# Earlier and later loads at three places of a decoder layer on one core

## The chip, the cores and the metric

The kernel runs on one core of one Trainium2 chip. The time is device microseconds of one execution; the median of three runs stands for a kernel. The engines are TensorE (PE, with its weight loads PEld), VectorE (DVE), ScalarE (ACT), GpSimd (POOL) and SyncE (SP). Each of them takes its instructions in a fixed order. SP does no arithmetic here: it issues most of the transfers (queue q1 of the profile). POOL issues the rest (queue q0).

## The reference

One decoder layer over 256 tokens of 2048 channels, in float32:

```
h = layer_norm(ALPHA * x + 0.5 * swiglu(x, w_gate1, w_up1, w_down1))       # norm 1
c_q, c_kv, k_r, dq, dk, dv, gate_mla, gate_diff = split(h @ w_in)
o_mla  = mla_attention(rms_norm(c_q) @ w_uq, rms_norm(c_kv) @ w_uk, ... @ w_uv)
o_diff = diff_attention(dq, dk, dv)
y      = sigmoid(gate_mla) * (o_mla @ w_br_mla) + sigmoid(gate_diff) * (o_diff @ w_br_diff)
h = layer_norm(ALPHA * h + y @ w_out)                                       # norm 2
h = layer_norm(ALPHA * h + 0.5 * swiglu(h, w_gate2, w_up2, w_down2))       # norm 3
```

The compressed rows are c_q and c_kv, 512 columns each, which go through an RMS norm and then into `w_uq`, `w_uk` and `w_uv`.

## The kernel before, in words

**Units.** All weights pass through the chip once, in units of two 128-row slices of 512 columns: 512 KB (`project`, L216). For each unit the kernel loads 128x1024 floats into a `raw` buffer (4 of them, SP issues, L235), splits them into a high and a low half (`split`, L153: ACT casts to the high half on L154, DVE subtracts it from the source on L155) into a pair of the ring (`wring`), and multiplies: each product of a 128x128 activation tile with 512 columns is three matmuls, high by high, high by low and low by high (`triple`, L207 to L210). A unit serves 256 tokens as two halves of 128, so `project` has 12 matmuls for each unit, 6 for a half. Where the products go through seven combined forms (`Hybrid`, L351), a unit of a form has 6.

**Order.** The order of work is set in three ways. First, the code is traced unit by unit: `unit` (L194) loads, and `advance` then prepares (casts) and multiplies units that are `look`ed ahead by a given number. Each unit multiplied is one tick; `later(n, fn)` (L103) puts a step n ticks on. Second, the framework plans a static order for each engine and queue from these instructions: one that is ready, and for which a buffer is free, may be placed ahead of others. Third, `tc.issue_after(ins)` puts an instruction behind `ins` on the same engine, in order only. `fetched[0]` is the last weight transfer traced.

**Buffers.** The `tmp` tag has 6 buffers of 128x512 floats, shared by everything that is short-lived: a row block on its way out (`blocks`), one on its way back (`turned`), rows of a product (`dkTr`), gain and shift rows (`gp`). A turn of a 128x512 block goes through DRAM: DVE transposes 32x32 blocks (L715), POOL stores them in four transfers (L717), and POOL reads them back in one (`turned`, L729 or L1227).

**The start.** `xT`, the transposed input, comes in four quads of 512 channels, for two token halves each (`load_x`, L1399; tile `xraw`, then split into `x`). `first_tokens` and `second_tokens` call it within the first projection of feed-forward 1. In that projection unit 0 is loaded and split in two halves (`parts`, L230), every other unit whole. Quad 0 serves units 0 and 1, quad 1 serves units 2 and 3.

**The compressed rows.** After their RMS norm, c_q and c_kv are stored turned. `c_back` (L1224), in the mixer, reads the four blocks back, 6 ticks after the `dk` projection has been traced; `cn.put` (L1231) splits them 12, 14, 16 and 18 ticks after. At that point seven units are loaded or cast and not yet multiplied. The `dv` projection, 22 units, lies between this and the first product with `cn` (`w_uq`).

**Norm 2.** While `w_out` is multiplied (4 column blocks of 512, 8 units each), the object `LayerNorm` (L739) prepares the residual. `rows` (L756, transfer on L764) loads rows of h, four blocks of 128x1024 (tile `z`), and `gained` (L766) loads the gain and shift rows of norm 1 for 512 columns (tile `gp`, the same 2 KB for all 128 partitions, transfer on L770), and multiplies, adds and scales (`use`, L772 to L777). The calls take their ticks from the constructor on L1425: rows at 1, 3, 11, 13; `gained` at 2, 7, 14, 21; `use` 4 and 6 ticks after `gained`. The transfers are put behind the last weight transfer traced. For the first columns `use` also waits until the last quad of y has been split (`past`). Just before, in the last branch projection (`om`), the merged rows `diff` are made by DVE (L1374 to L1376) and turned: two quads through DRAM (`turned`, split into `y`), the last two by PE with an identity matrix (L671).

Of the kernel before, what the change touches and what calls it, by code (L numbers as in the profile page):

```python
# [30 lines left out]
G = 2  # L31
# [28 lines left out]
def layer_kernel(ctx: ExitStack, tc: tile.TileContext, a: dict, out: bass.AP):  # L60
    nc = tc.nc
# [10 lines left out]
    def nm(s):  # L72
        uid[0] += 1
        return f"{s}_{uid[0]}"
# [10 lines left out]
    def mm_bank(name="mm"):  # L85
        return psum.tile([P, 512], F32, tag="mm", name=nm(name), bufs=5)
# [16 lines left out]
    def later(n, fn):  # L103
        uid[0] += 1
        heapq.heappush(todo, (step[0] + n, uid[0], fn))
# [42 lines left out]
            assert (k, b) in self.ready, (self.name, k, b)  # L148
            return self.tiles[k // 8, b][which][:, k % 8, :]

    cast, lows, fetched = [None], [None], [None]

    def split(hi, lo, src):  # L153
        cast[0] = S.copy(hi, src)  # L154
        lows[0] = V.tensor_tensor(out=lo, in0=src, in1=hi.bitcast(F32), op=ALU.subtract)  # L155
        return lows[0]
# [37 lines left out]
    def unit(load, prep, now, later_on=None):  # L194
        if load is not None:
            load()
        loaded.append((prep, now, later_on))
        advance(*ahead)

    def next_pair():  # L200
        assert len(ring) > len(prepared) + lag[0], (len(ring), len(prepared), lag[0])
        catch_up(len(ring) - 1)
        pair = ring.pop(0)
        ring.append(pair)
        return pair

    def triple(o, xh, xl, wh, wl, first, last, again=False):  # L207
        PE.matmul(o, xh, wh, start=first, stop=False, skip_group_check=again)  # L208
        PE.matmul(o, xh, wl, start=False, stop=False, skip_group_check=again)  # L209
        PE.matmul(o, xl, wh, start=False, stop=last, skip_group_check=again)  # L210

    def project(w, x, k_tiles, width, done, k0=0, hook=None, between=None, norm=None, free=(3, 7)):
        banks = [None, None]
        units = k_tiles // G

        def products(b, j, pair):  # L216
            if j == 0:
                banks[b] = mm_bank()
            o = banks[b][:, :width]
            wh, wl = pair  # L220
            for g in range(G):
                k = j * G + g
                xk = k0 + k
                triple(o, x.at(0, xk, b), x.at(1, xk, b), wh[:, g, :], wl[:, g, :], k == 0, k == k_tiles - 1)
            if j == units - 1:
                done(b, banks[b])

        def one(j):
            st = {}
            parts = [slice(i * width, (i + 1) * width) for i in range(G)] if between is not None and j == 0 else [slice(0, G * width)]  # L230

            def load():
                st["raw"] = wpool.tile([P, G * width], F32, tag="raw", name=nm("raw"), bufs=4)
                for c in parts:
                    fetched[0] = nc.sync.dma_start(st["raw"][:, c], w[j][:, c])  # L235

            def prep():
                pair = [t[:, :G * width] for t in next_pair()]
                waits = ()
                if norm is not None and j >= free[0]:  # L240
                    if j >= free[1]:
                        waits = norm.applied[1], norm.root[1]
                    else:
                        waits = norm.x.made[0, 0], norm.root[0] if j == free[0] else norm.x.cast[0, 0]
                with ExitStack() as stack:
                    for i in waits:
                        stack.enter_context(tc.issue_after(i.ins))
                    for c in parts:
                        split(*(t[:, c] for t in pair), st["raw"][:, c])
                st["pair"] = [t.rearrange("p (g n) -> p g n", g=G) for t in pair]  # L250
            def second():
                if between is not None:
                    between(j)
                products(1, j, st["pair"])
            return load, prep, lambda: products(0, j, st["pair"]), second

        for j in range(units):
            if hook is not None:
                hook(j)
            unit(*one(j))  # L260
# [459 lines left out]
    def turned(v):  # L720
        return v.rearrange("p (i k c) -> p k i c", i=4, k=4)
# [17 lines left out]
    class LayerNorm:  # L739
        def __init__(self, scale, residual, g, bt, each, x=None, cols=None, at=((0, 2, 4, 6), (8, 11, 14, 17)), ahead=None, pending=None, due=(), past=None):  # L740
            self.scale = scale
            self.ahead = ahead
            self.x = x
            self.cols = None
            if cols is not None:
                t = tmp_tile([P, 2, KD], "cols")
                nc.gpsimd.dma_start(t.rearrange("p a k -> p (a k)"), cols)
                self.cols = [t[:, i, :] for i in range(2)]
            self.each = each
            self.z = [[None, None] for _ in range(2)]  # L750
            self.counted = [0, 0]
            self.gb = [[None, None] for _ in range(2)]
            self.applied = {}
            self.root = []

            def rows(h, b):  # L756
                t = self.z[b][h] = act_tile([P, 1024], F32, "z")
                src = residual[b, :, h * 1024:(h + 1) * 1024]
                if pending is None:
                    nc.gpsimd.dma_start(t, src)  # L760
                    later(4, lambda: S.mul(t, t, ALPHA))
                else:
                    with tc.issue_after(fetched[0].ins):
                        nc.sync.dma_start(t, src)  # L764

            def gained(c):  # L766
                v = [tmp_tile([P, 512], "gp") for _ in range(2)]
                for t, src in zip(v, pending):
                    with tc.issue_after(fetched[0].ins):
                        nc.sync.dma_start(t, src[0:1, c * 512:(c + 1) * 512].partition_broadcast(P))  # L770

                def use(b):  # L772
                    z = self.z[b][c // 2][:, (c % 2) * 512:(c % 2) * 512 + 512]
                    with tc.issue_after((past() if past is not None and c == 0 else lows[0]).ins):
                        V.tensor_tensor(out=z, in0=z, in1=v[0], op=ALU.mult)
                    V.tensor_tensor(out=z, in0=z, in1=v[1], op=ALU.add)
                    S.mul(z, z, ALPHA)  # L777
                later(4, lambda: use(0))
                later(6, lambda: use(1))
            for c, n in enumerate(due):  # L780
                later(n, lambda c=c: gained(c))

            def vector(i, h):
                t = self.gb[i][h] = act_tile([P, 1024], F32, "gb")
                nc.gpsimd.dma_start(t, (g, bt)[i][0:1, h * 1024:(h + 1) * 1024].partition_broadcast(P))
            for n in range(4):
                later(at[0][n], lambda n=n: rows(n // 2, n % 2))
                if cols is None:
                    later(at[1][n], lambda n=n: vector(n // 2, n % 2))
            self.stats = [small.tile([P, 4, 6], F32, tag="bn", name=nm("bn"), bufs=4) for _ in range(2)]  # L790
# [340 lines left out]
    def mixer(x):  # L1131
# [4 lines left out]
        cn = Acts(8, "cn")  # L1136
# [66 lines left out]
        for i, f in ((0, 0), (1, 0), (0, 2)):  # L1203
            w = (a["wgm"], a["wgd"])[i]
# [17 lines left out]
        back = {}  # L1222

        def c_back():  # L1224
            for key, src in turns.items():
                back[key] = tmp_tile([P, 512], "turned")
                nc.gpsimd.dma_start(back[key], src)  # L1227
        later(6, c_back)
        for i in range(2):
            for b in range(2):  # L1230
                later(12 + 4 * i + 2 * b, lambda i=i, b=b: cn.put(i, b, turned(back[i, b])))  # L1231
        hy.group(a["wdv"][0], a["wdv"][1], lambda n, b, bank, snap, op: whole(
            dv[b][:, n * 512:(n + 1) * 512], bank, snap, op), False, True)
        look(0, 0)
# [125 lines left out]
        yq = Acts(KD, "y")  # L1360
# [34 lines left out]
    res = [dram.tile([2, P, D], F32, name=f"res{i}") for i in range(2)]  # L1395
# [2 lines left out]

    def load_x(q, b):  # L1399
        raw = xq.raw(q, b) if q in xq.kept else tmp_tile([P, 512], "xraw")  # L1400
        nc.sync.dma_start(raw, a["xT"][q, b])
        xq.put(q, b, raw.rearrange("p (k t) -> p k t", k=4))

    def first_tokens(j):
# [9 lines left out]
    def keep(i):  # L1414
        def each(b, c, z):
            nc.gpsimd.dma_start(res[i][b, :, c * 512:(c + 1) * 512], z)
        return each
# [4 lines left out]
    yq = mixer(h1)  # L1422
    narrow_to(6)
    h2 = Acts(KD, "h2", (0, 1, 2))
    ln = LayerNorm(1.0, res[0], a["ln2_g"], a["ln2_b"], keep(1), h2, a["ln2_cols"], ((1, 3, 11, 13), ()), 1,  # L1425
                   (a["ln1_g"], a["ln1_b"]), (2, 7, 14, 21), lambda: yq.made[3, 1])
    for c in range(4):
        project(a["w_out"][c], yq, KD, 512, lambda b, bank, c=c: ln.evac(c, b, bank),
                hook=at_unit(0, widen) if c == 3 else None)
# [90 lines left out]
```

## Time and profile before

| what | us |
|---|---|
| median of 3 runs | 1966.95 (1966.76 to 1967.8) |
| the profiled execution | 1969.03 |
| its span, first to last instruction | 1967.3 |

A row of the timeline gives the start, the duration, the engine, the line, the operation with its tiles (out<-in) and shapes, and a count; in square brackets stands how long the engine was idle before it, and on what. A matmul row can last longer than the distance to the next one, as matmuls are pipelined: the distance of the starts is what one costs. A row of the waits names the engine and the operation that waited, what it waited for, the sum in us, the number of times and the longest. A row of the windows gives, for a stretch, its length, the busy time of PE, PEld, DVE, ACT and POOL with the instructions of each, the granted clock of PE, the share of the transfer engines and GB/s. SPq and POOLq are the queues on which SP and POOL issue transfers.

### The profile page before, as it was taken

What the parts mean: (1) busy time and instruction counts of PE and PEld (TensorE: products, weight loads), DVE (VectorE), ACT (ScalarE), POOL (GpSimd) and SP (SyncE); (2) the same over time, 40 slices, a digit from 0 to 9 for tenths busy, and PEclk for the clock granted to TensorE, in tenths of its full rate; (3) what the DMA queues carried; (4) which work ended last, traced back from release to release, by engine and by line L of the source; (5) the groups of instructions that cost most, each with busy time, mean ns of one, the idle gap of its engine ahead of it and who ended that gap; (6) DMA issues with size and microseconds to landing.
All of it is one profiled execution on the core that took longest, in us unless ns stands there. A gap on an engine that the chain in (4) does not pass through costs nothing.

```text
span 1967.3 us, 25772 instructions
## 1 busy us (share of the span) xinstructions
PE 1951.7 (99%) x8760; PEld 1618.2 (82%) x8760; DVE 1777.8 (90%) x2183; ACT 1249.7 (64%) x1634; POOL 309.3 (16%) x531
## 2 busy tenths in 40 slices
PE   9999999999999999999999999999999999999997
PEld 8888888888888898888888887888888888888886
DVE  7999999998998879988987676789999999999986
ACT  6666766676655666666667654556676666765661
POOL 0112111122100010102241530001211112210000
PEclk9999999999999999999999999999999999999999
DMA  8978888878776666767685788678888878787773
GB/s 315 285 227 262 268 261 247 259 234 306 271 238 214 208 223 248 246 223 262 203 248 196 236 295 274 198 261 255 255 267 264 250 238 271 251 314 236 277 233 121
DMA packets 149779, 488.83 MB, mean 248 GB/s; under 512 B 21600, under 2 KB 21648, under 8 KB 149648
## 3 DMA queue, kind: packets, MB, share of 16 engines
q1 hardware_dynamic: 119088, 401.13, 59.5%
q0 software_dynamic: 30560, 86.07, 16.8%
q8 instruction: 68, 1.11, 0.2%
q14 instruction: 63, 0.52, 0.1%
HBM read 456.71 MB, written 30.41 MB: 248 GB/s over the span
## 4 chain that ended last, share of the span: by engine, by line
PE 92%; DMA 3%; DVE 1%; issue 1%; ACT 1%; POOL 1%; SPq 0%; DVEq 0%; POOLq 0%; ACTq 0%
PE mm L209 29%; PE mm L208 29%; PE mm L210 29%; DMA turned<-turn 1%; DMA gate<-gates 1%; PE tr L210 1%; PE tr L209 1%; PE tr L208 1%; DMA turn<-blocks 0%; POOL turn L717 0%; PE tr L671 0%; ACT wring L154 0%; DMA raw<-in_wgd_dram 0%; DMA raw<-in_gu_dram 0%; PE tr L1322 0%
## 5 line engine op out<-in xcount | busy, mean ns | idle before, releaser
L154 ACT CAST wring<-raw 128x1024 fp32r<-128x1024 f32 (+2 forms) x467 | 481.9, 1037 | 322.3 <-PE mm L210 236.7
L155 DVE TENSOR_TENSOR wring<-raw,wring 128x1024 fp32r<-128x1024 f32 (+2 forms) x467 | 557.4, 1201 | 91.7 <-ACT wring L154 89.4
L154 ACT CAST wring<-sraw 128x1024 fp32r<-128x1024 f32 x436 | 453.0, 1052 | 201.9 <-DVE sraw L428 85.7
L155 DVE TENSOR_TENSOR wring<-sraw,wring 128x1024 fp32r<-128x1024 f32 x436 | 520.7, 1219 | 23.6 <-ACT wring L154 20.7
L208 PE MATMUL mm<-wring,h 128*128 128x512 f32 (+2 forms) x1248 | 480.9, 385 | 0.0
L210 PE MATMUL mm<-wring,h 128*128 128x512 f32 (+2 forms) x1248 | 480.3, 385 | 0.0
L209 PE MATMUL mm<-wring,h 128*128 128x512 f32 (+2 forms) x1248 | 480.0, 385 | 0.0
L208 PE MATMUL mm<-wring,xs 128*128 128x512 f32 x776 | 302.2, 389 | 0.6 <-ACT snap L385 0.6
L209 PE MATMUL mm<-wring,xs 128*128 128x512 f32 x776 | 301.9, 389 | 0.0
L210 PE MATMUL mm<-wring,xs 128*128 128x512 f32 x776 | 301.9, 389 | 0.0
L208 PEld LDWEIGHTS mm<-wring,h 128*128 128x128 f32 x1248 | 234.5, 188 | 46.9 <-ACT h L154 0.6
L209 PEld LDWEIGHTS mm<-wring,h 128*128 128x128 f32 x1248 | 234.5, 188 | 46.5 <-DVE wring L155 0.4
L210 PEld LDWEIGHTS mm<-wring,h 128*128 128x128 f32 x1248 | 234.4, 188 | 46.5 <-DVE h L155 0.7
L428 DVE TENSOR_TENSOR sraw<-sraw,sraw 128x1024 f32<-128x1024 f32 x168 | 199.2, 1219 | 2.0 <-DMA sraw<-in_wgm_dram 1.2
L208 PEld LDWEIGHTS mm<-wring,xs 128*128 128x128 f32 x776 | 145.7, 188 | 31.2 <-ACT snap L385 1.0
L210 PEld LDWEIGHTS mm<-wring,xs 128*128 128x128 f32 x776 | 145.7, 188 | 30.2
L209 PEld LDWEIGHTS mm<-wring,xs 128*128 128x128 f32 x776 | 145.7, 188 | 30.1
L717 POOL DMA_DIRECT2D hT<-blocks x176 | 96.8, 562 | 367.0 <-DVE blocks L715 366.0
L209 PE MATMUL mm<-wring,x 128*128 128x512 f32 x336 | 130.8, 389 | 0.5 <-DVE wring L155 0.5
L208 PE MATMUL mm<-wring,x 128*128 128x512 f32 x336 | 130.8, 390 | 0.0
L210 PE MATMUL mm<-wring,x 128*128 128x512 f32 x336 | 130.6, 389 | 0.0
L430 POOL DMA_DIRECT2D sraw<-in_gu_dram x40 | 35.5, 889 | 371.3 <-DVE sraw L428 288.3
(310 smaller groups left out, 2286.7 us busy)
## 6 DMA issues: line engine op xcount, KB each, us to landing
sraw<-in_gu_dram SPq DMA_DIRECT2D x160, 512.0 KB, 5.2
raw<-in_gu_dram SPq DMA_DIRECT2D x159, 512.0 KB, 4.9
raw<-in_dn_dram SPq DMA_DIRECT2D x140, 512.0 KB, 4.7
sraw<-in_gu_dram POOLq DMA_DIRECT2D x40, 512.0 KB, 7.1
sraw<-in_dn_dram SPq DMA_DIRECT2D x36, 512.0 KB, 5.2
eraw<-in_gu_dram SPq DMA_DIRECT2D x64, 256.0 KB, 5.8
raw<-in_w_out_dram SPq DMA_DIRECT2D x32, 512.0 KB, 4.3
hraw<-hT POOLq DMA_DIRECT2D x56, 256.0 KB, 5.8
```

What stands on the lines that cost most here:

```text
L154: cast[0] = S.copy(hi, src)
L155: lows[0] = V.tensor_tensor(out=lo, in0=src, in1=hi.bitcast(F32), op=ALU.subtract)
L208: PE.matmul(o, xh, wh, start=first, stop=False, skip_group_check=again)
L209: PE.matmul(o, xh, wl, start=False, stop=False, skip_group_check=again)
L210: PE.matmul(o, xl, wh, start=False, stop=last, skip_group_check=again)
L428: last = V.tensor_tensor(out=R[src][i], in0=R[src][i], in1=R[add[1]][i], op=ALU.add)
L430: nc.gpsimd.dma_start(R["12"][s], source("22", s), accum_op=ALU.add)
L717: nc.gpsimd.dma_start(to.rearrange("(g r) (i f) -> i r g f", g=4, i=4)[i], t[32 * i:32 * (i + 1), :].rearrange("r (g f) -> r g f", g=4))
```

## The change

At the start, unit 1 too is loaded and split in halves, and unit 3's transfer is put behind the last transfer of x that has been traced (x's second quad). In the mixer, the reads of the compressed rows move from 6 to 12 ticks, and their splits from 12 to 18. In norm 2, the first two row loads move from ticks 1 and 3 to 2 and 4, the first two `gained` from 2 and 7 to 3 and 8; `use` of the first columns follows 3 and 5 ticks after instead of 4 and 6, so that it keeps its place.

```diff
-            parts = [slice(i * width, (i + 1) * width) for i in range(G)] if between is not None and j == 0 else [slice(0, G * width)]
+            parts = [slice(i * width, (i + 1) * width) for i in range(G)] if between is not None and j < 2 else [slice(0, G * width)]
...
-                for c in parts:
-                    fetched[0] = nc.sync.dma_start(st["raw"][:, c], w[j][:, c])
+                with tc.issue_after(placed[0].ins) if between is not None and j == 3 else nullcontext():
+                    for c in parts:
+                        fetched[0] = nc.sync.dma_start(st["raw"][:, c], w[j][:, c])
...
-                later(4, lambda: use(0))
-                later(6, lambda: use(1))
+                wait = 3 if past is not None and c == 0 else 4
+                later(wait, lambda: use(0))
+                later(wait + 2, lambda: use(1))
...
-        later(6, c_back)
+        later(12, c_back)
...
-                later(12 + 4 * i + 2 * b, lambda i=i, b=b: cn.put(i, b, turned(back[i, b])))
+                later(18 + 4 * i + 2 * b, lambda i=i, b=b: cn.put(i, b, turned(back[i, b])))
...
-        nc.sync.dma_start(raw, a["xT"][q, b])
+        placed[0] = nc.sync.dma_start(raw, a["xT"][q, b])
...
-    ln = LayerNorm(1.0, res[0], a["ln2_g"], a["ln2_b"], keep(1), h2, a["ln2_cols"], ((1, 3, 11, 13), ()), 1,
-                   (a["ln1_g"], a["ln1_b"]), (2, 7, 14, 21), lambda: yq.made[3, 1])
+    ln = LayerNorm(1.0, res[0], a["ln2_g"], a["ln2_b"], keep(1), h2, a["ln2_cols"], ((2, 4, 11, 13), ()), 1,
+                   (a["ln1_g"], a["ln1_b"]), (3, 8, 14, 21), lambda: yq.made[3, 1])
```

More of the change, by code (lines that the diff above doesn't have):

```diff
@@ L149, in at @@
             return self.tiles[k // 8, b][which][:, k % 8, :]
-    cast, lows, fetched = [None], [None], [None]
+    cast, lows, fetched, placed = [None], [None], [None], [None]
     def split(hi, lo, src):
```

## The prediction

> **What bounds the kernel now.** I read the page first, then the waits of TensorE, then the timeline around each of them.
>
> ```profile
> span 1967.3 us, 25772 instructions
> PE 1951.7 (99%) x8760; PEld 1618.2 (82%) x8760; DVE 1777.8 (90%) x2183; ACT 1249.7 (64%) x1634; POOL 309.3 (16%) x531
> ...
> PE tr L671 <- DVE diff L1376: 1.8, 1, 1.8
> ...
> PE mm L208 <- ACT snap L385: 0.6, 1, 0.6
> PE mm L209 <- DVE wring L155: 0.5, 1, 0.5
> ```
>
> TensorE (PE) is busy for 99% of the span, and everything else is cover for it. No row of PE work is added or removed by the change, so it can only win where PE waits, and that list is short. Beside two small ones that the diff does not touch it holds these three, and each lies beside one part of the change. Their real size is read from the starts of neighbouring matmuls:
>
> ```profile
> 9.20 0.63 PE L208 MATMUL mm<-wring,x 128*128 128x512 f32 x2
> 10.36 0.50 PE L209 MATMUL mm<-wring,x 128*128 128x512 f32 x1 [0.53 <-DVE wring L155]
> ...
> 957.67 0.39 PE L210 MATMUL mm<-wring,h 128*128 128x512 f32 x1
> 958.66 0.50 PE L208 MATMUL mm<-wring,xs 128*128 128x512 f32 x1 [0.61 <-ACT snap L385]
> ...
> 1185.03 0.39 PE L209 MATMUL mm<-wring,om 128*128 128x512 f32 x1
> 1185.25 0.39 PE L210 MATMUL mm<-wring,om 128*128 128x512 f32 x1
> 1187.49 0.63 PE L671 MATMUL tr<-ident,diff 128*128 128x128 f32 x4 [1.84 <-DVE diff L1376]
> ```
>
> Undisturbed matmuls start 0.23 us apart (1185.03, 1185.25). So the first wait costs 10.36-9.20-2x0.23 = 0.70 us, the second 958.66-957.67-0.23 = 0.76, the third 1187.49-1185.25-0.23 = 2.01. **Together 3.47 us, 0.18% of 1966.95.** That caps what the change can win; 0.2%, about what a measurement of this kernel can tell from no change, is 3.93 us.
>
> **Part A, the start.** Unit 1 of the weights is one 512 KB transfer, one cast (ScalarE, ACT) and one subtraction (VectorE, DVE); PE waits for that subtraction.
>
> ```profile
> 2.59 1.38 SPq L235 DMA_DIRECT2D raw<-in_gu_dram  x3
> 4.01 1.20 SPq L1401 DMA_DIRECT2D xraw<-in_xT_dram  x2
> ...
> 4.03 0.62 ACT L154 CAST wring<-raw 128x512 fp32r<-128x512 f32 x1
> 5.58 0.62 ACT L154 CAST wring<-raw 128x512 fp32r<-128x512 f32 x1 [0.93 <-DMA raw<-in_gu_dram]
> 7.99 1.05 ACT L154 CAST wring<-raw 128x1024 fp32r<-128x1024 f32 x1 [0.84 <-DMA raw<-in_gu_dram]
> 11.53 1.14 ACT L154 CAST x<-xraw 128x512 fp32r<-128x512 f32 x2
> ...
> 7.18 0.69 DVE L155 TENSOR_TENSOR x<-xraw,x 128x512 fp32r<-128x512 f32 x1 [0.26 <-ACT x L154]
> 9.07 3.81 DVE L155 TENSOR_TENSOR wring<-raw,wring 128x1024 fp32r<-128x1024 f32 x3 [1.20 <-ACT wring L154]
> 12.80 1.29 DVE L155 TENSOR_TENSOR x<-xraw,x 128x512 fp32r<-128x512 f32 x2
> ...
> 6.00:8.00 2.00, 2.00 (x10) 1.73 (x10) 1.39 (x2) 0.82 (x3) 0.00 (x0) 1.00 1.01 398
> ```
>
> The unit lands at 7.97, is cast to 9.04 and subtracted until 9.07+3.81/3 = 10.34. At 398 GB/s half a unit (262 KB) takes 0.66 us, so the first half lands at about 7.3 (an estimate) and is cast by 7.95; its subtraction (0.69) follows the one of x, which ends at 7.87, and is done at 8.65. The second half is cast 7.99 to 8.61 and done at 9.35. PE wants the first half at 9.20 and the second three matmuls later, at 9.88: both are there. Added are one SP issue (1.38/3 = 0.46 us, while landings trail the issues by five microseconds), 2x0.62-1.05 = 0.19 us of ACT and about 0.15 of DVE, both of which sat idle before 7.99 and 9.07. If that cover were gone, they would cost those 0.3 us.
>
> What is late next is x's second quad: PE would reach unit 2 0.7 us sooner, but those two transfers are issued after unit 3 (4.01) and cast at 11.53 only. The second edit orders unit 3 behind them, which brings them forward by 512 KB, 1.3 us, more than the 0.7 needed. Unit 3 itself is wanted two units of 12 matmuls (5.4 us) after 9.20 and can spare 1.3. So A removes the wait: **-0.7**, between -0.7 and +0.3 (the rival below).
>
> [...]
>
> **Part B, the compressed rows.** `c_back` (4 reads on POOL's queue into 4 of the 6 `tmp` buffers) and four `cn.put` (a cast and a subtraction each) go 6 ticks later.
>
> ```profile
> 949.45 0.62 ACT L154 CAST cn<-turned 128x512 fp32r<-128x512 f32 x1 [2.60 <-DMA turned<-turn]
> ...
> 958.03 0.58 ACT L385 COPY snap<-mm 128x512 f32<-128x512 f32 x1
> ...
> L154 ACT CAST cn<-turned x4: 613/616/621, 942.9 to 952.4; 128x512 fp32r<-128x512 f32 x4
> L155 DVE TENSOR_TENSOR cn<-turned,cn x4: 683/689/694, 950.4 to 964.1; 128x512 fp32r<-128x512 f32 x4
> ...
> 944.00:965.00 21.00, 20.36 (x89) 16.08 (x88) 20.04 (x23) 14.38 (x19) 7.30 (x14) 1.00 0.73 230
> 965.00:985.00 20.00, 20.00 (x90) 16.57 (x89) 16.47 (x15) 13.72 (x16) 1.09 (x2) 1.00 0.66 223
> ...
> 983.34 0.39 PE L208 MATMUL mm<-wring,cn 128*128 128x512 f32 x1
> ...
> 958.75 4.37 POOL L717 DMA_DIRECT2D turn<-blocks  x8 [12.36 <-DVE blocks L715]
> ```
>
> ACT is served in order. At 949.45 it had stood 2.60 us in front of a `cn` cast whose read had not landed; the weight casts behind it came late, and the snapshot that PE needs was copied at 958.03 instead of at once. In the same 21 us DVE was 95% busy (20.04), 4x0.69 = 2.8 us of it for `cn`. Moved into 965 to 985, where DVE has 3.5 us and ACT 6.3 us of idle time, these instructions fit, and the block goes. A unit here takes 1.4 or 2.7 us (6 or 12 matmuls), so 6 ticks are 8 to 16 us: the last subtraction, begun at 964.1, would be done by 981, ahead of the first use at 983.34. The four buffers are also free for `dkTr` and `blocks`, for which POOL stood 12.36 us. So **-0.8** (the 0.76); the other end is the slower rival below.
>
> **Part C, norm 2's first rows.** Two row loads, and the gain and shift (`gp`) of columns 0 and 1, are ordered one weight unit later on SP's queue; the arithmetic on column 0 keeps its tick, that of column 1 (4 DVE, 2 ACT instructions) moves one unit, to ticks 12 and 14, still two units ahead of the first sum of column 1 (unit 16). Here the question is whether a transfer truly moves.
>
> ```profile
> 1170.75 0.33 SPq L235 DMA_DIRECT2D raw<-in_w_out_dram  x1
> 1175.44 0.33 SPq L770 DMA_DIRECT2D gp<-in_ln_g_dram  x1
> 1175.87 0.90 SPq L235 DMA_DIRECT2D raw<-in_w_out_dram  x2
> ...
> 1179.39 0.33 SPq L235 DMA_DIRECT2D raw<-in_w_out_dram  x1
> 1179.77 0.93 SPq L764 DMA_DIRECT2D z<-res  x2
> 1180.81 0.42 SPq L770 DMA_DIRECT2D gp<-in_ln_g_dram  x1
> ...
> 1176.64 0.55 POOL L729 DMA_DIRECT2D turned<-turn  x1 [3.28 <-issue]
> 1183.66 0.62 ACT L154 CAST y<-turned 128x512 fp32r<-128x512 f32 x1 [4.55 <-DMA turned<-turn]
> ...
> DMA to landing us min/median/max: 2.9/4.3/7.0
> ...
> 1175.00:1178.00 3.00, 3.00 (x17) 2.47 (x16) 3.00 (x5) 2.48 (x4) 1.08 (x2) 1.00 0.39 109
> ```
>
> PE's 2.01 us come from the last `turned` read, issued at 1176.64 and landed at 1183.63; ACT stood 4.55 us before it, and DVE's L1376 came late. The line of landings, for all `turned` reads, shows this one as the slowest: 7.0 us, with a median of 4.3. Just ahead of it went the first `gp`, and in 1175 to 1178 the core moved only 109 GB/s. If `gp` moved behind it, the 2 us would go. But the order asked for is already kept: the column 0 loads had to follow units 0, 1 and 2 and in fact follow unit 3 (1170.75 is the fourth) or unit 6, since they wait for buffers. Only the pair of column 1, asked to follow unit 6 and issued right behind it at 1180.81, is truly held back, and it is issued after the read that is late. So **0**; the other end is -2.0.
>
> **Sum:** -0.7-0.8+0 = -1.5. The profiled execution took 1969.03 with a span of 1967.3; nothing of the change lies outside the span, so it would become 1967.5, and the median of the runs, 1966.95, becomes **1965.4**.
>
> **Rivals.**
> (1) *C works too:* the order of SP's queue is planned anew, the first `gp` falls behind the late read, and that lands after the median 4.3 us, 2.7 sooner, more than the 2.0 that PE waits: -1.5-2.0, **1963.4**. For it: `gp` waits for a buffer, and which is freed first can flip. Against: no edge of the diff asks for it.
> (2) *Halves in series or a stall that moves:* if unit 1's halves land as far apart as unit 0's (1.55 us), the second comes at 8.9 to 9.5, is done up to 10.9, and PE wants it at 9.88: up to 1.0 lost for 0.7 won. Likewise a `cn` cast can block ACT at another place for as long as now. Then +0.3 and 0: **1967.2**.
> (3) *Slower, by the reads of B:* they now come after the `blocks` stores in POOL's queue, which stood until 958.75 and took 4.37 us. If the reads are issued behind those, from 963.1, the last lands near 970, while ACT's casts are queued for earlier. Now a block of 4.55 us cost PE 2.0, so some 2.5 us are covered; a block of 10 us would cost 7.5. It eats A's 0.7 from 3.2 us of block on, and shows as slower by 0.2% from 2.5+0.7+3.9 = 7.1: with 10 it is 1966.95-0.7+7.5 = **1973.8**. Against it: the stores stood because the reads held the buffers.
> (4) *A small new wait from the replanned order*, of 1 to 4 us net, as C's is now: **1969**.
>
> **Chances.** Forecast 0.39 (1964.3 to 1966.2); (1) 0.27; (2) 0.16; (3) 0.09; (4) 0.09. Faster than 1963.0 needs all three waits gone (1963.5) and half a microsecond of smaller gaps besides: 0.05. Slower than 1970.9: (3) and a little of (4), 0.11. The range from 1962.9 to 1969.2 holds the forecast, (1), (2) and half of (4): 0.86.
>
> **What the profile will show.** A right: no wait of `mm L209` for `wring` before 11 us. B right: no wait for `snap L385` near 957, `cn` casts between 950 and 975, none idle for long before it. C as said: the wait of `tr L671` for `diff L1376` still there, near 1.8 us, behind a `turned` read of 7 us. Wrong would be a PE wait that is new, above all at the first `wring,cn` product.

## The result, and the profile after

| | kernel before | changed kernel |
|---|---|---|
| median, 14 runs each on one chip | 1967.58 us (1966.39 to 1969.16) | 1971.32 us (1969.93 to 1973.64) |
| profiled execution, its span | 1969.03, 1967.3 | 1971.49, 1969.7 |

The ratio is 1.0019, with a 95% interval of 1.0012 to 1.0027: **slower by 3.7 us** (2.4 to 5.3), where 1.5 us faster was forecast. The head of the page and the waits of TensorE (what waited for what: sum, times, longest) of the changed kernel:

```profile
span 1969.7 us, 25770 instructions
PE 1953.7 (99%) x8760; PEld 1617.7 (82%) x8760; DVE 1776.8 (90%) x2184; ACT 1249.6 (63%) x1635; POOL 309.5 (16%) x531
```

```profile
PE mm L209 <- DVE wring L155: 2.1, 4, 1.3
...
PE tr L1113 <- DVE p L1261: 0.8, 1, 0.8
PE mm L208 <- ACT wring L154: 0.7, 1, 0.7
```

(The changed file is one line longer behind L233 and two behind L778.) Two waits that the prediction spoke of, for `snap` and for `diff`, are not in this list. The waits for `wring` have grown from 0.5 to 2.8 us, and one for `p` from 0.3 to 0.8. The timeline of PE shows where:

```profile
31.30 0.39 PE L210 MATMUL mm<-wring,x 128*128 128x512 f32 x1
32.34 0.73 PE L208 MATMUL mm<-wring,x 128*128 128x512 f32 x2 [0.65 <-ACT wring L154]
34.38 0.50 PE L209 MATMUL mm<-wring,x 128*128 128x512 f32 x1 [1.30 <-DVE wring L155]
...
34.95 0.62 PE L208 MATMUL mm<-wring,x 128*128 128x512 f32 x1
...
37.92 0.60 PE L210 MATMUL mm<-wring,x 128*128 128x512 f32 x1
38.35 0.40 PE L208 MATMUL mm<-wring,x 128*128 128x512 f32 x1
```

Here, 20 us behind the edit, PE waits twice for one weight unit: 32.34-31.30-0.23 = 0.81 us for its cast and 34.38-32.34-2x0.23 = 1.58 for its subtraction. Then, from 34.95 to 38.35, matmuls start 0.43 us apart (37.92, 38.35) instead of 0.23. The windows around it (length, busy time of PE, PEld, DVE, ACT, POOL, granted clock, share of the transfer engines, GB/s) say why:

```profile
31.00:35.00 4.00, 2.04 (x9) 1.06 (x8) 4.00 (x4) 4.00 (x5) 0.00 (x0) 0.99 0.59 183
35.00:38.40 3.40, 3.40 (x10) 2.62 (x9) 3.40 (x4) 2.70 (x4) 0.00 (x0) 0.51 0.69 242
38.40:45.00 6.60, 6.60 (x31) 5.43 (x30) 4.56 (x5) 3.06 (x3) 0.00 (x0) 1.00 0.98 387
```

The granted clock was 0.51 for 3.4 us: 8 matmuls at 0.20 us more each, 1.6 us. DVE and ACT were both busy without a gap while PE stood. In the kernel before no two starts of PE between 11 and 60 us stand more than 0.2 us too far apart.

**How the wait comes about.** The unit that PE waits for is unit 1 of the second projection. These are the rows of ACT before it, in the changed kernel, and behind them the landing of that unit (the issue between 20.15 and 20.18 us on SP's queue, KB, us to landing):

```profile
26.43 1.06 ACT L154 CAST wring<-raw 128x1024 fp32r<-128x1024 f32 x1 [2.69 <-DMA raw<-in_gu_dram]
27.39 1.04 ACT L154 CAST xs<-fa 128x1024 fp32r<-128x1024 f32 x1
28.45 1.28 ACT L865 ACT_TABLE_LOAD   x1
29.75 0.66 ACT L865 ACTIVATE sg<-mm 128x256 f32<-128x256 f32 x2
30.29 3.00 ACT L154 CAST wring<-raw 128x1024 fp32r<-128x1024 f32 x3
```

```profile
raw<-in_gu_dram SPq DMA_DIRECT2D x1, 512.0 KB, 4.9
```

DVE's row for the subtractions of the three:

```profile
31.97 3.49 DVE L155 TENSOR_TENSOR wring<-raw,wring 128x1024 fp32r<-128x1024 f32 x3
```

And ACT in the kernel before:

```profile
25.43 1.06 ACT L154 CAST wring<-raw 128x1024 fp32r<-128x1024 f32 x1 [0.49 <-DMA raw<-in_gu_dram]
26.51 1.28 ACT L863 ACT_TABLE_LOAD   x1
27.95 0.38 ACT L863 ACTIVATE sg<-mm 128x256 f32<-128x256 f32 x1 [0.16 <-PE mm L210]
28.23 2.00 ACT L154 CAST wring<-raw 128x1024 fp32r<-128x1024 f32 x2
```

The timeline leaves the buffer numbers out; the static order that the framework planned for ACT has them (u0 to u4 are the units of the second projection, `fa` a cast of the combined forms):

```
before:  u0  fa  u2  table  SiLU 1  u1  u3  SiLU 2
changed: u0  u2  fa  table  SiLU 1  SiLU 2  u3  u1  u4
```

Before, u1 is the first of the two casts at 28.23 and done by 29.2. In the changed kernel it had landed at 20.16+4.9 = 25.06, but it is the second of three casts at 30.29, behind u2 (for which ACT stood 2.69 us), `fa`, the table, both SiLUs and u3: cast at 32.3, and on DVE subtracted behind u3 until 31.97+2x1.16 = 34.3. PE starts on it at 32.34 and 34.38. **The data was there; the order kept it.** Why the plan sets u1 behind u3 is not to be seen in a trace and stays open. Nothing in the diff names this cast. What the diff did name is seen on SP's queue, before and after:

```profile
4.01 1.20 SPq L1401 DMA_DIRECT2D xraw<-in_xT_dram  x2
6.95 0.33 SPq L235 DMA_DIRECT2D raw<-in_gu_dram  x1
7.32 0.91 SPq L1401 DMA_DIRECT2D xraw<-in_xT_dram  x2
```

```profile
4.01 1.16 SPq L1403 DMA_DIRECT2D xraw<-in_xT_dram  x2
5.21 4.43 SPq L236 DMA_DIRECT2D raw<-in_gu_dram  x3
9.69 0.90 SPq L1403 DMA_DIRECT2D xraw<-in_xT_dram  x2
```

Unit 3, the fourth, follows x's second quad, as ordered. But three units now stand between the two quads, where there was one: the fourth, the fifth, and the sixth, which came behind the third quad before. So x's third quad is issued at 9.69 instead of 7.32.

### The profile page after: what moved, and what is told of

Read it like the earlier page. It is cut to its first block, busy times and chain, and to the rows that moved or that the text cites. A ratio compares the mean times of both kernels' runs of the same rounds, so it can differ in the third digit from the quotient of the medians.

```text
span 1969.7 us, 25770 instructions
## 1 busy us (share of the span) xinstructions
PE 1953.7 (99%) x8760; PEld 1617.7 (82%) x8760; DVE 1776.8 (90%) x2184; ACT 1249.6 (63%) x1635; POOL 309.5 (16%) x531
## 4 chain that ended last, share of the span: by engine, by line
PE 95%; DMA 2%; DVE 1%; ACT 1%; issue 1%; POOL 0%; SPq 0%; DVEq 0%; ACTq 0%; POOLq 0%
PE mm L210 30%; PE mm L209 30%; PE mm L208 30%; PE tr L208 1%; PE tr L209 1%; PE tr L210 1%; DVE wring L155 1%; PE tr L672 0%; DMA raw<-in_gu_dram 0%; ACT wring L154 0%; DMA turned<-turn 0%; DMA raw<-in_wuq_dram 0%; DMA xraw<-in_xT_dram 0%; PE tr L1324 0%; PE tr L1326 0%
```

## The experiments

The theory after this reading (theory 1): the quad edge, the second edit of part A, is the whole loss, through the order planned around it. The rivals: the halves (theory 2), or only both edits together (theory 3). All comparisons are with the kernel before on the same chip.

| run | what | ratio | 95% interval | medians apart, us |
|---|---|---|---|---|
| e_quad | quad edge alone | 1.0021 | 1.0013 to 1.0030 | +4.0 |
| e_halves | halves alone | 1.0001 | 0.9992 to 1.0009 | +0.1 |
| e_late | parts B and C | 1.0000 | 0.9991 to 1.0009 | 0.0 |
| e_noquad | all but the quad edge | 1.0001 | 0.9992 to 1.0010 | -0.2 |
| e_order | changed kernel, sixth unit behind x's third quad | 1.0000 | 0.9991 to 1.0009 | 0.0 |
| e_silu | changed kernel, first SiLU behind the cast of u1 | 1.0003 | 0.9994 to 1.0012 | +0.3 |
| e_fill | changed kernel, PE kept at work in the wait | 1.0021 | 1.0012 to 1.0030 | +4.4 |
| e_norm | part C alone | 1.0000 | 0.9991 to 1.0009 | +0.2 |
| e_rows | part B alone | 1.0000 | 0.9992 to 1.0009 | +0.4 |
| e_start | part A alone | 1.0015 | 1.0006 to 1.0025 | +2.6 |

**The quad edge alone** (e_quad).

```diff
+                with tc.issue_after(placed[0].ins) if between is not None and j == 3 else nullcontext():
...
+        placed[0] = nc.sync.dma_start(raw, a["xT"][q, b])
```

> The second edit of part A alone: x's second quad is loaded ahead of the fourth unit; unit 1 is loaded whole, the compressed rows and norm 2 stay as before. Theory 1: this edit is the whole loss of the start. Ordering unit 3 behind the quad gives the planner another order: the first feed-forward's ScalarE casts unit 1 of its second projection behind both SiLUs, which themselves wait for TensorE, so TensorE runs dry for about 2 us between 31 and 35 us and then works for some 3.4 us at half the granted clock (0.51 in the changed kernel), about 1.6 us more. It should be 3 to 4.5 us slower than the kernel before and show both the wait and the clock. Theory 2 (the halves are the cause): about 0, within 0.7 us of before, with no wait of the product for a cast after 30 us. Theory 3 (only both edits together): about 0 here too.

Slower by 4.0 us: the whole loss, so theories 2 and 3 fall. Its waits of PE, and the windows of the wait and behind it:

```profile
PE mm L209 <- DVE wring L155: 2.3, 3, 1.3
...
PE mm L208 <- ACT wring L154: 0.8, 1, 0.8
```

```profile
32.50:36.20 3.70, 1.56 (x7) 0.66 (x5) 3.70 (x5) 3.70 (x5) 0.00 (x0) 1.00 0.49 167
36.20:40.00 3.80, 3.80 (x17) 3.15 (x18) 3.80 (x4) 3.23 (x4) 0.00 (x0) 1.00 0.93 282
```

The waits are those of the changed kernel, and the planned order of ACT is the same. One thing that was expected is missing: the clock stayed at 1.00. So the half clock is not part of the regular price.

**The halves alone** (e_halves).

```diff
-            parts = ... if between is not None and j == 0 else ...
+            parts = ... if between is not None and j < 2 else ...
```

> The first edit of part A alone: unit 1 is loaded in halves, everything else as before. Theory 1: the casts at 20 to 35 us keep the order of the kernel before, so between -0.7 us and +0.3 us. Theory 2 (the halves are the cause): 3 to 4 us slower, with the wait of the product for a cast between 31 and 35 us. Theory 3 (only both edits together): about 0.

No change (+0.1). The old wait behind 9.20 us is gone from its profile, and PE instead waits at 12.91 us for x's second quad. By the starts that is 12.91-11.99-0.23 = 0.69 us, as much as the wait that went (0.70):

```profile
PE mm L208 <- ACT x L154: 0.5, 1, 0.5
```

**Parts B and C without A** (e_late) **and all but the quad edge** (e_noquad).

```diff
 # e_noquad: the changed kernel, less
-                with tc.issue_after(placed[0].ins) if between is not None and j == 3 else nullcontext():
```

> Parts B and C without part A: the compressed rows split six units later, norm 2's first rows one unit later, the start as before. Theory 1: TensorE's lag on the changed kernel's trace falls by 0.3 us over the compressed rows and by 1.8 us over norm 2, so 2.0 to 2.8 us faster than before, with the waits near 957 and 1185 us gone. The prediction's sum for these two parts: 0.8 us faster, with the wait at 1185 us left.

> The changed kernel without the order of x's second quad ahead of the fourth unit: halves of unit 1, compressed rows six units on, norm 2's first rows one unit on. Theory 1: 2.0 to 3.4 us faster than the kernel before, so faster than both kernels, at about 1964.5 us. Theory 2 (the halves are the cause): 1 to 2.5 us slower than before. Theory 3 (only both edits of part A together): as theory 1.

Both come out level with the kernel before (0.0 and -0.2). Theory 1 is right that the loss goes with the edge, and wrong that a gain is left: the 2.0 to 2.8 us that I had read off two traces do not exist in the medians. Why not is shown by the next runs.

**The order put right in two ways** (e_order, e_silu).

```diff
 # e_order
-                with ... if between is not None and j == 3 else nullcontext():
+                with ... if between is not None and j in (3, 5) else nullcontext():
 # e_silu, in gu_done of feed-forward 1
+            if n == 1 and c == 0:
+                def held():
+                    with tc.issue_after(unit_casts[1].ins):
+                        half(c, b, bank[:, 256:512], bank[:, 0:256])
+                later(3, held)
+                return
```

> The changed kernel with one more order: the sixth unit is loaded behind x's third quad, as the fourth is behind the second. Planned this way, the third quad stands ahead of the sixth unit again on SyncE's queue, as in the kernel before, and ScalarE casts unit 1 of the second projection behind one SiLU instead of behind both SiLUs and units 2 and 3. Theory 1 (the quad edge loses only through the order that the planner makes of it): the wait at 31 to 34 us and the half clock go, 2.5 to 4.5 us faster than the changed kernel, between -1.5 and +0.7 us against the kernel before. Rival (the transfers are late whatever ScalarE's order: ScalarE itself waited 2.7 us for a weight unit at 26.4 us in the changed kernel): 2 to 4 us slower than before, with a wait of the product for a cast in the second projection still there.

> The changed kernel with the SiLU of the first block put three steps later and behind the cast of unit 1 of the second projection; SyncE's order of loads, the late third quad included, stays that of the changed kernel. Theory 1a (the loss is that cast's place behind the SiLUs): the wait at 31 to 34 us goes or shrinks below 0.5 us, no half clock, 2.5 to 4 us faster than the changed kernel, between -1 and +1 us against the kernel before. Rival (the late loads themselves): 2 to 4 us slower than before.

Both give the loss back, as far as their intervals tell. e_silu is the sharper one: x's third quad is as late as in the changed kernel (issued at 9.43), ACT stands as long for u2 (2.94 us), and what differs is ACT's order behind it. u1 is cast ahead of the table and of both SiLUs; the second SiLU and the cast of `fb` have other places too. Its ACT rows, and the start of u1's products on PE:

```profile
26.54 1.05 ACT L154 CAST wring<-raw 128x1024 fp32r<-128x1024 f32 x1 [2.94 <-DMA raw<-in_gu_dram]
...
28.45 1.04 ACT L154 CAST wring<-raw 128x1024 fp32r<-128x1024 f32 x1
29.51 1.28 ACT L867 ACT_TABLE_LOAD   x1
```

```profile
31.15 0.39 PE L210 MATMUL mm<-wring,x 128*128 128x512 f32 x1
31.38 0.61 PE L208 MATMUL mm<-wring,x 128*128 128x512 f32 x2
31.83 0.39 PE L209 MATMUL mm<-wring,x 128*128 128x512 f32 x1
```

u1 is cast at 28.45, ahead of the table, and PE goes through at 0.23 us a matmul. Late loads without the late cast come out at +0.3 us (interval -1.2 to +2.4) and without the wait; the rival that blamed the transfers had 2 to 4 us slower, and falls. e_order, with all of part A's edits and a better order, has hardly a wait left (beside this line only the wait for `zero` ahead of the first product, 1.1 us in every profile, and 0.2 us for `p`):

```profile
PE mm L209 <- DVE wring L155: 0.8, 3, 0.3
```

and still its median is that of the kernel before (1967.59; the profiled execution took 1966.42).

**PE kept at work in the wait** (e_fill).

```diff
+            if late:            # last product of unit 0 of the second projection
+                t = tr_bank()
+                with tc.issue_after(placed[1].ins):
+                    for i in range(fill):     # 6
+                        PE.matmul(t[:, 0:P], zero, zero, start=True, stop=True)
```

> The changed kernel with six products of a zero tile (about 0.37 us each by the first rows of the trace) between the products of units 0 and 1 of the second projection, into a bank that nobody reads: the wait for the cast stays, but TensorE works through it. Theory 1b (the half clock at 35 to 38 us follows from TensorE standing idle at 31.7 to 34.4 us): the granted clock stays near 1.0 there and 1.6 us come back, so 1.3 to 1.9 us faster than the changed kernel and about 2 us slower than before. Rival (the half clock has another cause): as the changed kernel, 3.5 to 4.2 us slower than before, with spacing of 0.43 us between products again.

```profile
32.05 1.50 PE L233 MATMUL tr<-zero 128*128 128x128 f32 x12
33.31 0.71 PE L208 MATMUL mm<-wring,x 128*128 128x512 f32 x2
35.04 0.50 PE L209 MATMUL mm<-wring,x 128*128 128x512 f32 x1 [1.02 <-DVE wring L155]
35.38 0.40 PE L210 MATMUL mm<-wring,x 128*128 128x512 f32 x1
35.62 0.40 PE L208 MATMUL mm<-wring,x 128*128 128x512 f32 x1
```

The spacing behind the wait is 0.23 us, but nothing came back: +4.4 us, where theory 1b had about 2 and the rival 3.5 to 4.2 (the rival's spacing of 0.43 us did not come either). The six products took 1.26 us (twelve rows, as such a product is two) and not 2.2, and a wait of 1.27 us (35.04-33.31-2x0.23) was left behind them. The list of executions says more: their mean clock was 0.997 in 5 of 14 executions of the changed kernel, 3 of 11 of e_quad and 2 of 11 of e_start; in none of 11 of e_fill, in 1 of 11 of e_order and in 1 of the 87 of the kernel before that ran beside the experiments. In the changed kernel the five averaged 1972.6 us and the nine others (0.998) 1970.7. So the lower clock goes mostly with the unfilled wait, in some executions, and explains scatter of 1 to 2 us, not the 3.7. The clocks are given to 0.001, and 3.4 us at half clock are 0.0009 of the span, so which executions had it cannot be counted surely.

**Norm 2 alone** (e_norm).

```diff
-    ln = LayerNorm(..., ((1, 3, 11, 13), ()), 1, ..., (2, 7, 14, 21), ...)
+    ln = LayerNorm(..., ((2, 4, 11, 13), ()), 1, ..., (3, 8, 14, 21), ...)
```

> Part C alone: norm 2's first rows one unit on; start and compressed rows as before. Theory N1 (the wait of 1.84 us for norm 2's difference at 1187 us belongs to the one profiled execution of the kernel before, since two kernels with the same norm 2 showed 0.2 us and none): the time within 1 us of before. Theory N2 (the wait is in most executions of the kernel before, and part C removes it): 1.5 to 2 us faster. The prediction: 0, with the wait left.

No change (+0.2): N1. The wait of 1.84 us for `diff` at 1187 us was the one execution that had been profiled. Of the five profiles with norm 2 as before, that one shows it, e_quad shows the line below, and e_halves, e_rows and e_start none; the profiles with part C show none.

```profile
PE tr L672 <- DVE diff L1377: 0.2, 1, 0.2
```

**The compressed rows alone** (e_rows) **and the start alone** (e_start).

```diff
 # e_rows
-        later(6, c_back)
+        later(12, c_back)
...
-                later(12 + 4 * i + 2 * b, lambda i=i, b=b: cn.put(i, b, turned(back[i, b])))
+                later(18 + 4 * i + 2 * b, lambda i=i, b=b: cn.put(i, b, turned(back[i, b])))
```

> Part B alone: the compressed rows are read back and split six units later; start and norm 2 as before. The prediction: 0.8 us faster, because TensorE no longer waits for a snapshot near 957 us. Theory B1 (the wait is moved, not removed): that wait (0.8 to 1.0 us) is gone, but the vector work of the split now stands ahead of the mask product p of the second head, for which TensorE waits near 998 us; from the first product with the compressed rows to the second head's p 0.2 to 1.6 us are lost, and the time is within 1 us of before. Of norm 2, which is here as before: if its wait at 1187 us belongs to single executions, it may be anything from 0 to 2 us in this profile.

> Part A alone, both edits; compressed rows and norm 2 as before. Theory 1: the loss of the changed kernel is all here, so 3.5 to 4.5 us slower than before, with the waits of the product for casts near 18 and at 31 to 36 us. Theory 2 (parts B and C lose as well, and the quad order only in part): 2 us slower or less. Theory 1c (the half clock seen in the changed kernel's profile is chance and not the regular price): the granted clock may be 1.00 all through here, with the time no better for it.

Part B alone is level (+0.4). The `snap` wait is gone from its profile, as from every profile with part B; those without it have it (0.6, 0.8, 0.8, 0.9 and 0.8 us). What ACT does is not what the prediction had: it still stands in front of a `cn` cast, for 4.9 to 5.5 us in the seven profiles with part B against 2.6 to 2.9 without, but no snapshot that PE waits for stands behind that cast any more. In e_rows:

```profile
964.30 0.62 ACT L154 CAST cn<-turned 128x512 fp32r<-128x512 f32 x1 [5.22 <-DMA turned<-turn]
```

In place of the `snap` wait come waits for the second head's `p`, near 999 us. First DVE in the kernel before, then in e_rows:

```profile
988.27 0.56 DVE L1092 SCALAR_TENSOR_TENSOR st<-tr,bias 128x384 f32<-128x384 f32 x1 [0.61 <-PE tr L1250]
...
996.33 0.73 DVE L1259 SCALAR_TENSOR_TENSOR p<-p,rs,p 128x128 f32<-128x128 f32 x2
```

```profile
988.52 1.28 DVE L1194 TENSOR_TENSOR dv<-mm,snap 128x512 f32<-128x512 f32 x2
989.72 1.22 DVE L155 TENSOR_TENSOR wring<-raw,wring 128x1024 fp32r<-128x1024 f32 x1
990.85 0.55 DVE L1092 SCALAR_TENSOR_TENSOR st<-tr,bias 128x384 f32<-128x384 f32 x1
...
998.90 0.73 DVE L1259 SCALAR_TENSOR_TENSOR p<-p,rs,p 128x128 f32<-128x128 f32 x2
```

From the first product with `cn` (983.34 us before, 984.54 in e_rows) to `p` it took 996.33-983.34 = 13.0 us before and 998.90-984.54 = 14.4 now. Before, DVE stood idle for the products that `st`, the head of the chain to `p`, reads: they start at 987.42, and `st` follows after 0.85 us. In e_rows they start at 988.62, and DVE first does a pair of `dv` sums (1.28 us) and a weight subtraction (1.22), so that `st` follows after 2.23 us. Between the first product with `cn` and the following head's `p` on PE (near 1016 us), 32.1 us pass in all five profiles without part B and 32.2 to 33.7 in the seven with it (mean 32.6); from the transposes near 683 us to the first product with `cn` the mean is 0.2 us less with it, in profiles that scatter by about 1 us. So the wait was moved, as B1 had it, but not by the vector work of the split itself, whose last subtraction in e_rows begins at 975.26; it is weight subtractions and `dv` sums, put later, that now fall into the chain.

Part A alone is slower by 2.6 us, less than theory 1 had (3.5), with an interval (1.2 to 4.9 us) that holds the changed kernel too. Its waits, with no half clock in this profile (theory 1c):

```profile
PE mm L209 <- DVE wring L155: 1.7, 3, 1.3
...
PE mm L208 <- ACT wring L154: 1.0, 1, 1.0
```

## Why the prediction was wrong

**Part A (-0.7; measured +2.6 alone).** The failed step is the costing of the second edit: "Unit 3 itself is wanted two units of 12 matmuls (5.4 us) after 9.20 and can spare 1.3. So A removes the wait". That was true of unit 3 and was the wrong question. The edge gave the framework another plan, in which one more unit passes ahead of x's third quad and, 20 us on, one cast falls behind both SiLUs; that cast cost 2.4 us of waits, and one for unit 4 near 18 us 0.4. The other statements of this part held: the halves do remove the wait behind 9.20, what is late next is x's second quad (0.69 us in e_halves), and with both and a better order (e_order) neither wait is left. The halves did not come apart either: in the changed kernel the casts of unit 1's halves follow one another without a gap (from 7.32 us, 1.25 us for both), where those of unit 0's start 1.61 us apart (4.16 and 5.77).

But the 0.7 us does not appear in the medians of e_halves, e_noquad or e_order (+0.1, -0.2, 0.0). The profiles show where it goes. The first product with `xs` (a combined form, near 50 us on PE) has as many products ahead of it in every kernel but e_fill, which has its six more. It starts at 49.44 to 49.97 us (mean 49.69) in the four profiles whose start is as before, at 50.10 and 50.21 with the halves alone, at 52.39 to 53.53 in the four with the late cast, and at 48.65 and 49.06 in e_order and e_silu. So the loss is made within the first 50 us, the halves alone win nothing, and where both edits stand without the late cast PE is 0.6 to 1.0 us ahead. That is one execution each, and the medians of these two (0.0, +0.3) do not show it; whether most executions have it is open.

**Part B (-0.8; measured +0.4 alone, interval 0.9992 to 1.0009).** The wait was traced to the right cast, and it went in all seven profiles with the edit. The stall of ACT did not go with it, though: it grew to 5 us and only moved past the snapshot. What failed is taking the removal of the wait for a gain: "these instructions fit, and the block goes". They fit by their sums over 20 us, but the stretch from 985 to 999 holds a chain (mask, maximum, exponent, `p`) in which DVE's order counts, and there PE waits 0.2 to 1.6 us for `p`, where none of the five profiles without part B has a wait.

**Part C (0; measured +0.2).** Right, and for the reason given: the edit holds back little (in e_norm only the `gp` pair of column 1 falls behind one more unit, at 1184.68 us). But "the wait of `tr L671` for `diff L1376` still there, near 1.8 us" was wrong: I took a wait of one execution for a property of the kernel. It was also 2.0 of the 3.47 us that the prediction called the cap, and carried the rival (1), which had 0.27.

**The rivals.** What happened is the fourth: a small new wait from the replanned order, of 1 to 4 us net, at 1969. It had 0.09, priced at 2 us. It was listed for completeness and not looked for: I did not follow what the edge lets pass on SP's queue. Of the others, (1) rested on the wait of one execution, (2) on halves that come apart, which they did not, and (3) on a block of ACT, which came with 5 us and cost PE no wait there.

The half clock of the changed kernel's profile lasted 38.35-34.95 = 3.40 us; the clock records of its trace change at 4.22, 34.94 and 38.35 us. In the 3.4 us ahead of 34.95 PE had the two matmuls at 32.34 and two from 34.38, 4x0.23 = 0.92 us of work, 27%. The same wait does not always bring it: in the profiles of e_quad and e_start the clock stayed at 1.00. What decides between the two was not shown.

## What to carry to other kernels

An ordering edge in a kernel whose queues are planned as a whole is a change to every queue: before it is costed by what it moves, the planned order of before and after must be laid side by side, on the queues and engines that it does not name too, and every weight cast that falls behind a dependent activation must be priced. A wait is only worth removing if the stretch that takes over the work has no chain of its own. And a wait of 2 us that is seen in one profile of a kernel whose executions scatter by 3 us may belong to that execution alone; a second profile tells.

## What the runs showed of the hardware

**The start.** PE's first work are 12 products of a zero tile (L98, 24 rows), which nothing delays. Timeline rows of a stretch near 4.5 us, first in the kernel before, then in the changed kernel:

```profile
4.21 1.27 PE L98 MATMUL tr<-zero 128*128 128x128 f32 x5
```

```profile
4.33 1.06 PE L98 MATMUL tr<-zero 128*128 128x128 f32 x8
```

Five rows in 1.27 us and eight in 1.06 (0.21 and 0.11 us from start to start): in the changed kernel's profile these products ran twice as fast from about 4 us on, in that of before to the end not at all, though the granted clock is listed as 1.00 for both. The list has no earlier record than the first one of full clock, which stands at 4.22 us in the changed kernel's trace and at 6.50 in that of before. In e_fill the same product took 1.26/6 = 0.21 us, two rows of 0.105, which is the fast rate. So the first real product starts at 5.25 in the one and at 6.20 in the other, and at 5.16 and 6.20 in e_late and e_noquad: one microsecond of scatter per execution that no part of the change touches. At the first product with `xs`, near 50 us, it is no longer there: e_late starts earliest and comes to it at 49.97, the kernel before starts 1.04 us later and comes to it at 49.51.

**The clock behind a wait.** A wait of 2.4 us, broken by two matmuls, was followed by 3.4 us at a granted clock of 0.51 in the changed kernel's profile, while a wait of the same form in the profiles of e_quad and e_start was followed by a clock of 1.00 (from 32.50 to 40.00 us and from 30.00 to 42.00, the wait included), as was a wait of 2.0 us in that of the kernel before, at 1185 us (1.00 from 1187.4 to 1191).
